# Gate norm vector folded into the gate weights, its root applied at the sigmoid, p loaded later, and a 19-buffer weight ring started earlier

## The chip, the cores and the metric

One Trainium2 chip, one core. The metric is device time in microseconds of one execution of the whole program. All arrays are float32 in HBM; nothing is prepared on the host.

## The reference, cut to what matters

One layer on 1024 tokens of width 1024. The token mixers ahead of the experts are not touched by the change and are left out here.

```python
def rmsnorm(x, g):
    return x * lax.rsqrt(jnp.mean(x * x, axis=-1, keepdims=True) + EPS) * g

def reference(x, p, norm_mix, w_in, ...):
    ...                                        # mixers; h = h + concat(y_lru, y_gdn) @ w_out
    h = h + hier_moe(rmsnorm(h, norm_ffn[l]), w_router_group[l], ..., w_exp_gate[l], w_exp_up[l], w_exp_down[l])
    gate = jax.nn.sigmoid(rmsnorm(h, norm_ple[l]) @ w_ple_gate[l])
    h = h + gate * (p[l] @ w_ple[l])
    return rmsnorm(h, norm_final)
```

`hier_moe` has 32 experts of 1024 to 512 to 1024 (silu gate times up, then down); each token goes to two of them. `norm_ple` is the vector that the change folds: `rmsnorm(h, g) @ W` is `(h @ (g[:, None] * W))` times one number per token, the reciprocal root.

## The kernel before

Tokens are in 8 tiles of 128 rows. Four stages matter here.

**Output projection and routing (to about 600 us).** For each token tile c the loop makes h, its norm (`ffn_xn`, which writes the normed rows to HBM as `xn_d`), the router's logits and its choice. SP issues the loads and stores of this stage in program order, one queue: the store of h (`h_d`), the store `xn_d`, and between them pieces of the experts' weights.

**The weight stream.** `halves` is a list of 198 pieces of 1 MB, in the order in which they are used: two gate and two up pieces of an expert, two down pieces, and at the end w_ple, p and four pieces of w_ple_gate. `raw_half(n)` (L1130) issues n of them on SP into a ring of buffers, `ring_tile()`. The ring has 18: 6, and from the output projection's end 9 more (`MORE`), and from the experts on 3 more (`LATE`). A DMA on SP waits until the DMA eight places ahead of it has landed, and for its buffer's last reader. The last tile's `ffn_xn` store and `raw_half(MORE - 1)` stand behind that tile's norm. Then SP, as the other engines, comes to a branch on a value that routing computes (`further`, L1404 and L1405), and waits there both for the value and for all of its own DMAs.

**Experts.** For expert e rows are gathered by GpSimd's indirect DMA (`gather`, L1222) out of `xn_d`, transposed, and multiplied by gate, up (L1314) and down pieces; results are scattered to `y_d` (L1280), row by row, one row per slot and token.

**The p stage and the gate stage.** `p_T` transposes a tile of p and splits it in a high and a low part; `parts(w)` does the same to weights (ScalarE copies to the rounded type fp32r, L1524, and VectorE subtracts, L1525); `mm3` (L205) multiplies high by high, low by high and high by low. For each tile, `p @ w_ple` comes first, kept in ring buffers. In between, the tail reads the two expert results of each token (`y_load`), adds them (`y_sum`, L1615, on GpSimd but for tile 0), adds h (`y_add`, L1619), squares with a sum (`y_sq`, ScalarE L1625) and applies the norm (`y_norm`: a Newton root, L43 to L53, and L1631, which multiplies by the root and the vector gple). `split_T` (L1293 to L1295) transposes the result and splits it; per tile two half products follow (`gated`: sigmoid L1688, times p's product on GpSimd L1689; `added` L1692; `squared` L1695; and `last`, the final norm, with L1706 and the store). Within a tile's first half VectorE also runs `last` of the tile before, the split of the next tile and `y_norm` of the tile two further on.

From the output projection on, the engines' orders are written by hand; only the first stage is ordered by a scheduler.

Of the kernel before, what the change touches and what calls it, by code (L numbers as in the profile page):

```python
# [37 lines left out]

def newton_rsqrt(nc, pool, x, n, tag):

    r = pool.tile([P, n], F32, tag=tag + "_r")
    t = pool.tile([P, n + (n == 1)], F32, tag=tag + "_t")
    nc.vector.tensor_scalar(r.bitcast(I32), x.bitcast(I32), -0.5, 0x5F3759DF, op0=OP.mult, op1=OP.add)  # L43
    if n == 1:
        t, m = t[:, 0:1], t[:, 1:2]
        nc.vector.tensor_scalar(m, x, -0.5, None, op0=OP.mult)
    for _ in range(3):
        if n == 1:
            nc.vector.scalar_tensor_tensor(t, r, m, r, op0=OP.mult, op1=OP.mult)  # L49
# [34 lines left out]
def layer(ctx, tc, x, p, norm_mix, w_in, lru_conv_w, lru_conv_b, lru_wa, lru_ba, lru_wi, lru_bi,  # L84
# [70 lines left out]
    for k in range(0, KT, 2):  # L155
# [3 lines left out]
    VEC = ((lru_conv_w, 16), (gdn_conv_w, 48), (lru_conv_b, 4), (lru_ba, 4), (lru_bi, 4), (lru_lambda, 4),  # L159
           (lru_out_norm, 4), (gdn_out_norm, 1), (norm_ffn, 8))  # L160
    NV = sum(n for _, n in VEC)
    vrow = zp.tile([NV, P], F32, name="vrow")
    r0, vecs = 0, []
    for a, n in VEC:
# [4 lines left out]
    cvg = vec[:, 16:64].rearrange("p (j g) -> p j g", j=4)  # L169
    cvb, ba_, bi_, lam, lon, gon, gfc = (vec[:, 64:68], vec[:, 68:72], vec[:, 72:76], vec[:, 76:80],  # L170
                                         vec[:, 80:84], vec[:, 84:85], vec[:, 85:93])
    alog = cst.tile([P, NH], F32, name="alog")
# [791 lines left out]

    def ffn_xn(c, eng):
        xn, ht = xns[c], by_tile(prepared[c][2])
        xk, gk = (a.rearrange("p (k q) -> p k q", k=KT) for a in (xn, gffn))
        if eng is nc.scalar:
            eng.activation(xk, ht, AF.Copy, scale=rss[c])
            nc.gpsimd.tensor_mul(xn, xn, gffn)  # L970
        else:
            eng.scalar_tensor_tensor(xk, ht, rss[c], gk, op0=OP.mult, op1=OP.mult)
        nc.sync.dma_start(xn_d[c * P:(c + 1) * P, :], xn)

# [131 lines left out]
    for e in range(NE + 1):  # L1106
# [3 lines left out]
        if e == NE - 1:  # L1110
            halves += [wpe, p[0, 0].rearrange("(t p) c -> p t c", p=P)]
        if e > 0:
            halves += [wd_v[EXPERTS[e - 1], :, 2 * j:2 * j + 2, :] for j in range(2)]
    halves += [wpg[:, 2 * i:2 * i + 2, :] for i in range(4)]
    halves.reverse()
# [90 lines left out]
    ffn_logits(c, 1)  # L1206
    raw_half()
    ffn_lgs(c)
    step(cur, 2)
    ffn_xn(c, nc.vector)  # L1210
    raw_half(MORE - 1)
    r = route(c - 1, c + 1)
# [72 lines left out]

    def split_T(pool, src, n, tag, bufs=2, size=0):

        th = pool.tile([P, size or n, P], F32R, tag=tag + "h", bufs=bufs)
        tl = pool.tile([P, size or n, P], F32R, tag=tag + "l", bufs=bufs)
        for k0 in range(0, n, 4):  # L1290
# [74 lines left out]
    mo = ctx.enter_context(tc.tile_pool(name="mo", bufs=2, reuse_waits="tile"))  # L1365
    LATE = 3
    ring[0:0] = [(mo, f"w{i}") for i in range(LATE)]
# [139 lines left out]
    def p_T():  # L1507

        t = len(pp)
        if t % 4 == 0:  # L1510
            pr[:] = [mo.tile([P, KT, P], F32R, tag="x" + c, bufs=2, name="pt") for c in "hl"]
        ph, pl = (x[:, 2 * (t % 4):2 * (t % 4) + 2] for x in pr)
# [7 lines left out]

    def parts(w):

        wh, wl = ring_tile(F32R), ring_tile(F32R)
        nc.scalar.activation(wh, w, AF.Copy)  # L1524
        nc.vector.tensor_sub(wl, w, wh)  # L1525
        return wh, wl

# [3 lines left out]
    for e in range(NE + 1):  # L1531
# [49 lines left out]
        if e == NE - 1:  # L1581
            gple = xg2[0]
            nc.sync.dma_start(gple, bcast_rows(norm_ple, D))
            we = [a.rearrange("p (k c) -> p k c", k=2) for a in parts(wpr)]
            hr = ring_tile()
            for t in range(2):
                hs[t] = hr[:, t * D:(t + 1) * D]
                nc.sync.dma_start(hs[t], h_d[t])
            for t in range(4):
                p_T()  # L1590
    mst.close()
# [3 lines left out]

    with tc.tile_pool(name="tl", bufs=2, reuse_waits="tile") as tl:
        gfin = xg2[1]
        nc.sync.dma_start(gfin, bcast_rows(norm_final, D))
# [3 lines left out]
        y0s, y1s, sss, x2s = {}, {}, {}, {}  # L1602
        yr = None

        def y_load(t):
            if t < NT:
                y0 = tl.tile([P, D], F32, tag="y0", bufs=3)
                y1 = yr[:, (t % 2) * D:(t % 2) * D + D]
                y0s[t], y1s[t] = y0, y1
                for m, y in enumerate((y0, y1)):  # L1610
                    nc.sync.dma_start(y, y_d[m * S + t * P:m * S + (t + 1) * P, :])
# [14 lines left out]

        def y_norm(t):
            if t < NT:
                nc.vector.tensor_scalar(sss[t], sss[t], EPS, None, op0=OP.add)
                rs = newton_rsqrt(nc, sm, sss[t], 1, "nx")  # L1630
                nc.vector.scalar_tensor_tensor(y0s[t], hs[t], rs, gple, op0=OP.mult, op1=OP.mult)  # L1631

        for t in range(NT):
            if t < 4:
                p_T()
            ph, pl = pp[t]
            if t % 2 == 0:
                w = ring_tile()
                if t == 0:
                    yr = ring_tile()  # L1640
                pws[t], pws[t + 1] = w[:, 0:D], w[:, D:]
# [7 lines left out]
            if t == 0:  # L1649
                y_load(0)  # L1650
                y_load(1)
            if t in (1, 2, 3, 4):
                gw.append([a.rearrange("p (k c) -> p k c", k=2) for a in parts(wgr[t - 1])])
            if t == 4:
                y_sum(0, nc.vector)
                y_add(0)
                y_sq(0)
                y_sum(1)
                y_load(2)
            if t == 5:  # L1660
                y_norm(0)
        for t in range(2, NT, 2):
            w = ring_tile()
            for j in range(2):
                hs[t + j] = w[:, j * D:(j + 1) * D]
                nc.sync.dma_start(hs[t + j], h_d[t + j])
        x2s[0] = split_T(mo, y0s[0], KT, "x")
        y_load(3)
        y_add(1)
        y_sq(1)  # L1670
        y_sum(2)
        y_norm(1)
        y_add(2)
# [8 lines left out]
        def gated(t, n, ns, pg):  # L1682
# [4 lines left out]
            sg = sgs[t, n] = sg[:, 0:ns.stop - ns.start]  # L1687
            nc.scalar.activation(sg, pg, AF.Sigmoid)  # L1688
            (nc.vector if (t, n) >= (NT - 1, 1) else nc.gpsimd).tensor_mul(sg, sg, pws[t][:, ns])  # L1689
# [27 lines left out]
        for t in range(NT):  # L1717
            xh, xl = x2s[t]
            for n, ns in enumerate(pieces(t)):
# [4 lines left out]
                if n == 0:  # L1724
                    if t > 0:
                        last(t - 1)
                    if t + 1 < NT:
                        x2s[t + 1] = split_T(mo, y0s[t + 1], KT, "x")
                    y_load(t + 4)
                    added(t, 0, ns)  # L1730
                    y_norm(t + 2)
                    y_sum(t + 3)
# [39 lines left out]
```

## Time and profile before

| what | value |
|---|---|
| three runs | 1301.15, 1294.4, 1297.95 us |
| median | 1297.95 us |
| profiled execution, its own time | 1297.76 us |
| its span | 1296.1 us |
| mean granted TensorE clock | 0.962 |

The span is the time from the first to the last instruction in the trace; 1.66 us of the execution's time lie around it. Positions in the text are microseconds from the span's start. The busy lines give for each engine its busy time, share and count; the line of 40 slices gives one digit for each 32.4 us.

### The profile page before, as it was taken

Reading aid. Unit: us, or ns where it says so; the run is one execution under the profiler, and the core shown is the slowest. Engines: PE = TensorE matmul, PEld = TensorE weight load, DVE = VectorE, ACT = ScalarE, POOL = GpSimd, SP = SyncE. Lnnn points to the kernel's source line nnn. Section 1 sums busy time; section 2 is a strip of 40 time slices with the busy share of each in tenths; the row PEclk is TensorE's granted clock in tenths of the full one; section 3 lists DMA queues with packets and bytes.
Section 4 is the critical chain, followed back from the end, with each engine's and each line's share of the span. In section 5 each row is a group of like instructions: output and inputs, shape, how many; then the busy total and the mean of one; then the engine's idle time right before and its main releaser. Section 6 shows DMA issues by size and latency. Waiting matters only on the chain. (4 is left out here: it accounts for less than half of the span.)

```text
span 1296.1 us, 17798 instructions
## 1 busy us (share of the span) xinstructions
PE 1188.2 (92%) x6295; PEld 736.7 (57%) x6295; DVE 698.4 (54%) x1462; ACT 407.0 (31%) x691; POOL 265.5 (20%) x232
## 2 busy tenths in 40 slices
PE   6999979999889999975999999999999899998886
PEld 5987757776679988863333333333333333366665
DVE  7657766779878986883222212222222122266885
ACT  5423436654423234431121111111121122254232
POOL 2121224542141202221011111111111101012322
PEclk9999989999979999976999999999999999998998
DMA  6711121330544446668999999999999999864221
GB/s 206 251 33 50 36 54 66 98 82 0 151 132 147 147 145 214 247 231 352 401 398 397 384 401 389 399 390 395 395 397 390 377 392 404 351 249 174 98 82 49
DMA packets 98204, 309.43 MB, mean 239 GB/s; under 512 B 23423, under 2 KB 45020, under 8 KB 73501
## 3 DMA queue, kind: packets, MB, share of 16 engines
q1 hardware_dynamic: 91740, 290.74, 60.4%
q0 software_dynamic: 6336, 17.05, 3.9%
q8 instruction: 74, 1.21, 0.4%
q14 instruction: 54, 0.43, 0.1%
HBM read 273.28 MB, written 38.54 MB: 241 GB/s over the span
## 5 line engine op out<-in xcount | busy, mean ns | idle before, releaser
L1314 PE MATMUL b<-w,x 128*64 128x512 f32 x1024 | 235.8, 602 | 11.4 <-PEq L1545 4.7
L1314 PEld LDWEIGHTS b<-w,x 128*64 128x64 f32 x1024 | 72.6, 137 | 149.2 <-issue 141.3
L1314 PE MATMUL b<-w,h 128*64 128x512 f32 x512 | 124.2, 604 | 3.6 <-PEq L1567 2.9
L1326 DVE SCALAR_TENSOR_TENSOR gs<-gs,gts,b 64x512 f32<-64x512 f32 x32 | 23.7, 739 | 151.0 <-ACT gs L1325 144.2
L205 PE MATMUL b<-xh,wh 128*128 128x512 f32 x320 | 85.9, 411 | 0.0
L1222 POOL DMA_INDIRECT xg<-xn_d,idx x32 | 31.0, 969 | 263.9 <-PE b L1485 243.3
L205 PE MATMUL b<-xh,wl 128*128 128x512 f32 x320 | 79.2, 390 | 0.0
L205 PE MATMUL b<-xl,wh 128*128 128x512 f32 x320 | 79.0, 389 | 0.0
L1280 POOL DMA_INDIRECT y_d<-y,idx x32 | 29.5, 921 | 225.3 <-ACTq L1545 123.3
L286 POOL TENSOR_TENSOR wl<-w,wh 128x1024 fp32r<-128x1024 f32 x20 | 52.7, 2637 | 104.2 <-ACT wh L285 101.0
L1314 PEld LDWEIGHTS b<-w,h 128*64 128x64 f32 x512 | 33.2, 136 | 70.2 <-issue 55.4
L205 PEld LDWEIGHTS b<-xh,wh 128*128 128x128 f32 x320 | 61.9, 195 | 15.4 <-issue 1.7
L205 PEld LDWEIGHTS b<-xh,wl 128*128 128x128 f32 x320 | 60.3, 189 | 12.7
L205 PEld LDWEIGHTS b<-xl,wh 128*128 128x128 f32 x320 | 60.1, 188 | 12.5
L205 PE MATMUL b<-w,th 128*128 128x512 f32 (+1 forms) x272 | 66.0, 390 | 0.0
L1325 ACT ACTIVATE gs<-b 64x512 f32<-64x512 f32 x32 | 19.0, 595 | 126.6 <-PE b L1314 126.6
L1352 DVE TENSOR_TENSOR gs<-b,gs 32x512 f32<-32x512 f32 x13 | 8.9, 685 | 89.8 <-ACT yo L1351 89.8
L205 PEld LDWEIGHTS b<-w,th 128*128 128x128 f32 x272 | 49.6, 192 | 10.9 <-ACT th L1294 0.2
L1332 ACT ACTIVATE y<-b 64x512 f32<-64x512 f32 x32 | 19.0, 594 | 111.7 <-DVE y L1331 83.2
L1342 PE MATMUL b<-w,x 128*32 128x512 f32 x416 | 50.0, 598 | 3.3 <-PEq L1539 3.3
L1331 DVE COPY y<-b 64x512 f32<-64x512 f32 x32 | 21.9, 683 | 53.6 <-PE b L1314 50.1
L355 DVE SCALAR_TENSOR_TENSOR kq<-pre,vec,kq 128x1024 f32<-128x1024 f32 x24 | 47.0, 1958 | 0.9
(392 smaller groups left out, 2180.8 us busy)
## 6 DMA issues: line engine op xcount, KB each, us to landing
w<-in_w_exp_gate_dram SPq DMA_DIRECT2D x64, 1024.0 KB
w<-in_w_exp_up_dram SPq DMA_DIRECT2D x64, 1024.0 KB
w<-in_w_exp_down_dram SPq DMA_DIRECT2D x64, 1024.0 KB
w<-in_w_in_dram SPq DMA_DIRECT2D x20, 512.0 KB
xt<-in_x_dram SPq DMA_DIRECT2D x16, 512.0 KB
h_d<-xt SPq DMA_DIRECT2D x8, 512.0 KB
ht<-h_d SPq DMA_DIRECT2D x8, 512.0 KB
h_d<-ht SPq DMA_DIRECT2D x8, 512.0 KB
```

Source lines behind the costliest of these rows:

```text
L205: nc.tensor.matmul(o, a(k), b(k), start=(i == 0), stop=(i == 3 * n - 1))
L286: nc.gpsimd.tensor_sub(wl, raw[i], wh)
L355: nc.vector.scalar_tensor_tensor(dst, pre[:, t0 + j:t0 + j + n], w[:, j, g:g + 1], dst, op0=OP.mult, op1=OP.add)
L1222: nc.gpsimd.indirect_dma_start(out=xg[rows], out_offset=None, in_=xn_d[:], in_offset=bass.IndirectOffsetOnAxis(ap=idx[rows], axis=0), boun ...
L1280: i = nc.gpsimd.indirect_dma_start(out=y_d[:], out_offset=bass.IndirectOffsetOnAxis(ap=idx[rows], axis=0), in_=y[rows], in_offset=None, bo ...
L1314: nc.tensor.matmul(pb[rows], xT[:, k], of(k, m), start=(k == 0), stop=(k == n - 1))
L1325: nc.scalar.activation(dst, pb[other(r)], AF.Silu)
L1326: nc.vector.scalar_tensor_tensor(dst, dst, gt, pb[r], op0=OP.mult, op1=OP.mult)
L1331: nc.vector.tensor_copy(y[:, 0:512], pb[r])
L1332: nc.scalar.activation(y[:, 512:], pb[other(r)], AF.Copy)
L1342: nc.tensor.matmul(pb[32 * j:32 * j + 32], xT[:, k], of(k, m), start=(k < 2), stop=(k >= n - 2), tile_position=(0, 32 * j))
L1352: nc.vector.tensor_add(dst, pb[32:64], dst)
```

## The change

- `raw_half(MORE)` issues its nine pieces right behind the last tile's transposes, ahead of that tile's logits and norm; before, one piece stood behind the logits and eight behind the norm's store. The last tile's `xn_d` store is issued by ScalarE's queue in place of SP's.
- `LATE` is 4: the ring has 19 buffers. The room comes from the low parts (`xl`), which go to the tail's pool.
- p stands behind the last down pieces in the stream; its transposes are no longer inside the last expert's code but three ahead of the p stage and one in each of its tiles.
- `norm_ple` is loaded as columns (`gpl`) and applied when w_ple_gate is split: `parts(w, g)` runs two scaled copies on ScalarE and two scalar_tensor_tensor on VectorE of 1024 columns for each piece, where there was one of each of 2048. The broadcast of the vector to 128 rows (0.5 MB, L1583) is gone. The splits stand at tiles 0, 1, 4, 5 instead of 1 to 4.
- `y_norm` becomes `y_rs`: the root alone. L1631 is gone; `split_T` reads h itself, and the root is the sigmoid's scale on ScalarE.
- The expert results of a tile go to ring buffers, three pairs; `y_sum(0)` and `y_add(0)` move from the p stage's tile 4 to tile 2, `y_sq(0)` to 3, `y_sum(1)` to 5.

```diff
@@ ffn_xn
-    def ffn_xn(c, eng):
+    def ffn_xn(c, eng, queue=nc.sync):
...
-        nc.sync.dma_start(xn_d[c * P:(c + 1) * P, :], xn)
+        queue.dma_start(xn_d[c * P:(c + 1) * P, :], xn)
@@ halves
         if e == NE - 1:
-            halves += [wpe, p[0, 0].rearrange("(t p) c -> p t c", p=P)]
+            halves.append(wpe)
         if e > 0:
             halves += [wd_v[EXPERTS[e - 1], :, 2 * j:2 * j + 2, :] for j in range(2)]
+    halves.append(p[0, 0].rearrange("(t p) c -> p t c", p=P))
@@ end of the output projection
     for t in xg2:
         nc.gpsimd.memset(t, 0.0)
+    raw_half(MORE)
     step(cur)
...
     ffn_logits(c, 1)
-    raw_half()
     ffn_lgs(c)
     step(cur, 2)
-    ffn_xn(c, nc.vector)
-    raw_half(MORE - 1)
+    ffn_xn(c, nc.vector, nc.scalar)
@@ ring
-    LATE = 3
+    LATE = 4
@@ parts
-    def parts(w):
+    def parts(w, g=None):
         wh, wl = ring_tile(F32R), ring_tile(F32R)
-        nc.scalar.activation(wh, w, AF.Copy)
-        nc.vector.tensor_sub(wl, w, wh)
-        return wh, wl
+        if g is None:
+            nc.scalar.activation(wh, w, AF.Copy)
+            nc.vector.tensor_sub(wl, w, wh)
+        else:
+            for k in range(2):
+                ks = slice(k * D, k * D + D)
+                nc.scalar.activation(wh[:, ks], w[:, ks], AF.Copy, scale=g[:, k:k + 1])
+                nc.vector.scalar_tensor_tensor(wl[:, ks], w[:, ks], g[:, k:k + 1], wh[:, ks],
+                                               op0=OP.mult, op1=OP.subtract)
+        return [a.rearrange("p (k c) -> p k c", k=2) for a in (wh, wl)]
@@ tail
-        def y_norm(t):
+        def y_rs(t):
             if t < NT:
                 nc.vector.tensor_scalar(sss[t], sss[t], EPS, None, op0=OP.add)
-                rs = newton_rsqrt(nc, sm, sss[t], 1, "nx")
-                nc.vector.scalar_tensor_tensor(y0s[t], hs[t], rs, gple, op0=OP.mult, op1=OP.mult)
+                sss[t] = newton_rsqrt(nc, tl, sss[t], 1, "ny", bufs=4)
...
-            if t in (1, 2, 3, 4):
-                gw.append([a.rearrange("p (k c) -> p k c", k=2) for a in parts(wgr[t - 1])])
-            if t == 4:
+            if t in (0, 1, 4, 5):
+                i = len(gw)
+                gw.append(parts(wgr[i], gpl[:, 2 * i:2 * i + 2]))
+            if t == 2:
                 y_sum(0, nc.vector)
                 y_add(0)
+                y_load(2)
+            if t == 3:
                 y_sq(0)
+            if t == 5:
                 y_sum(1)
-                y_load(2)
-            if t == 5:
-                y_norm(0)
...
-        x2s[0] = split_T(mo, y0s[0], KT, "x")
+        x2s[0] = split_T(hs[0])
+        y_rs(0)
...
-            nc.scalar.activation(sg, pg, AF.Sigmoid)
+            nc.scalar.activation(sg, pg, AF.Sigmoid, scale=sss[t])
```

SP at the end of the output projection, before (`xn_d<-xn` is the store of normed rows, `w<-in_w_exp...` a piece of weights, L1404 the value that the branch waits for):

```order
L973 DMA xn_d<-xn 128x1024
L930 DMA h_d<-ht 128x1024
L1130 DMA w<-in_w_exp_gate_dram 128x2048
L973 DMA xn_d<-xn 128x1024
L1130 DMA w<-in_w_exp_up_dram 128x2048
L1130 DMA w<-in_w_exp_down_dram 128x2048 x2
L1130 DMA w<-in_w_exp_gate_dram 128x2048
L1130 DMA w<-in_w_exp_up_dram 128x2048
L1130 DMA w<-in_w_exp_gate_dram 128x2048
L1130 DMA w<-in_w_exp_up_dram 128x2048
L1130 DMA w<-in_w_exp_down_dram 128x2048
L1404 TENSOR_LOAD novi
```

The same place of SP now:

```order
L973 DMA xn_d<-xn 128x1024
L930 DMA h_d<-ht 128x1024
L1131 DMA w<-in_w_exp_gate_dram 128x2048
L1131 DMA w<-in_w_exp_up_dram 128x2048
L1131 DMA w<-in_w_exp_down_dram 128x2048 x2
L1131 DMA w<-in_w_exp_gate_dram 128x2048
L1131 DMA w<-in_w_exp_up_dram 128x2048
L1131 DMA w<-in_w_exp_gate_dram 128x2048
L1131 DMA w<-in_w_exp_up_dram 128x2048
L1131 DMA w<-in_w_exp_down_dram 128x2048
L1407 TENSOR_LOAD novi
```

The last store of normed rows no longer stands between the pieces; it is on ScalarE's queue.

VectorE through the p stage and into the gate stage, before (L1518 is p's low part, L1525 a weight's low part, L1615 and L1619 `y_sum(0)` and `y_add(0)`):

```order
L1518 TENSOR_TENSOR pt<-b,pt 128x256
L1525 TENSOR_TENSOR w<-w 128x2048
L1518 TENSOR_TENSOR pt<-b,pt 128x256
L1525 TENSOR_TENSOR w<-w 128x2048
L1518 TENSOR_TENSOR pt<-b,pt 128x256
L1525 TENSOR_TENSOR w<-w 128x2048 x2
L1615 TENSOR_TENSOR y_11680<-y_11680,w 128x1024
L1619 TENSOR_TENSOR w<-w,y_11680 128x1024
L1629 TENSOR_SCALAR ss<-ss 128x1
```

The same stretch of VectorE now (L1521 and L1534 are the low parts, L1625 and L1629 `y_sum(0)` and `y_add(0)`, L1298 the low part of tile 0):

```order
L1521 TENSOR_TENSOR xl<-b,xh 128x256 x4
L1534 SCALAR_TENSOR_TENSOR w<-w,vec 128x1024 x2
L1521 TENSOR_TENSOR xl<-b,xh 128x256
L1534 SCALAR_TENSOR_TENSOR w<-w,vec 128x1024 x2
L1521 TENSOR_TENSOR xl<-b,xh 128x256
L1625 TENSOR_TENSOR w<-w 128x1024
L1629 TENSOR_TENSOR w<-w 128x1024
L1521 TENSOR_TENSOR xl<-b,xh 128x256 x2
L1534 SCALAR_TENSOR_TENSOR w<-w,vec 128x1024 x4
L1298 TENSOR_TENSOR xl<-b,xh 128x512 x2
```

Tile 0's sum stands ahead of the second pair of weight splits, and its split (L1298) comes ahead of its root, with no norm in front of it.

VectorE inside one tile of the gate stage, from the end of the root to the next tile's final norm, before (L1631 is the norm of the gate's input, L1619 `y_add`, L1692 `added`, L1697 the final norm's mean; numbers behind a name are buffers):

```order
L53 SCALAR_TENSOR_TENSOR r<-t,r 128x1
L1631 SCALAR_TENSOR_TENSOR y_11877<-w,r,xg_5118 128x1024
L1619 TENSOR_TENSOR w<-w,y_11944 128x1024
L1692 TENSOR_TENSOR w<-w,sg 128x512
L1697 SCALAR_TENSOR_TENSOR ss<-ss 128x1
```

And now:

```order
L53 SCALAR_TENSOR_TENSOR r<-t,r 128x1
L1629 TENSOR_TENSOR w<-w 128x1024
L1701 TENSOR_TENSOR w<-w,sg 128x512
L1706 SCALAR_TENSOR_TENSOR ss<-ss 128x1
L43 TENSOR_SCALAR r<-ss 128x1
```

The multiply of 128x1024 is gone; the rest of the tile keeps its order.

## Rows read from the trace of the kernel before

**Rows 1.** The page, parts 1 and 2: busy time of TensorE and VectorE over the span, and in 40 slices the granted clock and the DMA share, in tenths.

```profile
PE 1188.2 (92%) x6295; PEld 736.7 (57%) x6295; DVE 698.4 (54%) x1462; ACT 407.0 (31%) x691; POOL 265.5 (20%) x232
...
PEclk9999989999979999976999999999999999998998
DMA  6711121330544446668999999999999999864221
```

**Rows 2.** Busy time by stretch, two answers of the windows view: columns are the stretch, its length, busy time of PE, PEld, DVE, ACT and POOL with counts, granted clock, DMA share, GB/s.

```profile
570.00:579.00 9.00, 7.33 (x32) 6.98 (x32) 6.50 (x29) 0.20 (x1) 0.89 (x2) 0.50 0.64 231
579.00:583.00 4.00, 0.00 (x0) 0.00 (x0) 3.52 (x21) 0.21 (x1) 0.00 (x0) 0.50 0.90 291
583.00:600.00 17.00, 7.17 (x32) 6.92 (x32) 10.79 (x53) 0.20 (x1) 4.12 (x5) 0.50 1.01 419
```

```profile
900.00:1000.00 100.00, 96.74 (x515) 32.93 (x512) 25.51 (x40) 20.14 (x36) 12.23 (x13) 1.00 1.02 395
1140.50:1165.00 24.50, 23.71 (x105) 18.69 (x104) 16.60 (x16) 14.34 (x19) 3.30 (x2) 1.00 0.56 214
1165.00:1175.00 10.00, 2.41 (x10) 2.11 (x11) 6.55 (x12) 5.10 (x10) 2.34 (x1) 0.61 0.91 356
1181.44:1193.90 12.46, 12.25 (x58) 9.72 (x57) 8.56 (x15) 5.22 (x9) 4.95 (x3) 1.00 0.24 84
1193.90:1208.90 15.00, 12.54 (x56) 9.69 (x57) 13.21 (x26) 4.43 (x10) 4.94 (x3) 1.00 0.30 105
1238.78:1253.73 14.95, 12.54 (x57) 9.69 (x57) 13.16 (x26) 4.43 (x10) 4.96 (x3) 1.00 0.09 37
1253.73:1266.56 12.83, 12.26 (x56) 9.75 (x57) 11.04 (x26) 4.43 (x10) 2.59 (x2) 1.00 0.10 41
```

**Rows 3.** SP's timeline ahead of the experts: start, length, what is issued. The length of a group of two runs to the end of the second.

```profile
569.97 0.78 SPq L1130 DMA_DIRECT2D w<-in_w_exp_gate_dram  x1
578.62 0.32 SPq L973 DMA_DIRECT2D xn_d<-xn  x1
...
583.36 24.22 SPq L1130 DMA_DIRECT2D w<-in_w_exp_down_dram  x2
607.70 0.35 SPq L1130 DMA_DIRECT2D w<-in_w_exp_gate_dram  x1
```

**Rows 4.** What SP's queue waits for from 560 to 615 us: who waits, for whom, us in total, times, longest.

```profile
SPq L1405 <- SPq L1405: 12.6, 3, 5.6
...
SPq L973 <- DVE xn L972: 7.8, 1, 7.8
```

**Rows 5.** What TensorE waits for from 600 to 1150 us, same columns.

```profile
PE b L1485 <- DMA xg<-xn_d,idx: 10.4, 1, 10.4
...
PE b L1314 <- DMA w<-in_w_exp_up_dram: 4.4, 3, 3.3
```

**Rows 6.** TensorE's timeline late in the experts, two of those waits: start, length, instruction, in brackets the idle time before it and what ended it.

```profile
1008.48 1.08 PE L1314 MATMUL b<-w,x 128*64 128x512 f32 x4 [3.26 <-DMA w<-in_w_exp_up_dram]
```

```profile
1026.21 1.08 PE L1314 MATMUL b<-w,x 128*64 128x512 f32 x4 [0.95 <-DMA w<-in_w_exp_up_dram]
```

**Rows 7.** GpSimd's timeline: the first gather; and of the DMA view of 565 to 610 us the gathers' median time from issue to landing, in us.

```profile
591.20 1.16 POOL L1222 DMA_INDIRECT xg<-xn_d,idx  x1 [20.31 <-DVE nb L1255]
```

```profile
xg<-xn_d,idx POOLq DMA_INDIRECT x3, 9.3
```

**Rows 8.** VectorE's timeline from the p stage into the gate stage.

```profile
1156.29 2.29 DVE L1525 TENSOR_TENSOR w<-w 128x2048 fp32r<-128x2048 f32 x1 [0.42 <-ACT w L1524]
1159.07 4.54 DVE L1525 TENSOR_TENSOR w<-w 128x2048 fp32r<-128x2048 f32 x1 [0.49 <-ACT w L1524]
1163.53 1.21 DVE L1615 TENSOR_TENSOR y<-y,w 128x1024 f32<-128x1024 f32 x1
...
1171.16 1.28 DVE L1631 SCALAR_TENSOR_TENSOR y<-w,r,xg 128x1024 f32<-128x1024 f32 x1
...
1196.80 0.16 DVE L1697 SCALAR_TENSOR_TENSOR ss<-ss 128x1 f32<-128x1 f32 x1 [1.23 <-ACT b L1695]
```

**Rows 9.** TensorE's timeline from the last p product to the second gate product.

```profile
1162.73 2.26 PE L205 MATMUL b<-w,pt 128*128 128x512 f32 x9
1172.59 1.94 PE L1293 MATMUL b<-ident,y 128*128 128x128 f32 x8 [7.60 <-DVE y L1631]
1174.37 3.50 PE L205 MATMUL b<-w,th 128*128 128x512 f32 x8
...
1181.44 1.04 PE L1293 MATMUL b<-ident,y 128*128 128x128 f32 x8
1182.23 2.11 PE L205 MATMUL b<-w,th 128*128 128x512 f32 x8
1184.18 2.03 PE L205 MATMUL b<-w,tl 128*128 128x512 f32 x8
```

**Rows 10.** GpSimd's timeline in the p stage: the sum of tile 1's expert results; and TensorE's: a pair of p's transposes in the last expert.

```profile
1159.06 2.39 POOL L1615 TENSOR_TENSOR y<-y,w 128x1024 f32<-128x1024 f32 x1 [14.06 <-DMA w<-y_d]
```

```profile
1141.28 0.44 PE L1515 MATMUL b<-ident,w 128*128 128x128 f32 x2 [0.78 <-DVE pt L1518]
```

**Rows 11.** What TensorE waits for from 1181 to 1285 us, the gate stage without its start.

```profile
PE b L1293 <- DVE y L1631: 6.0, 6, 1.3
PE b L205 <- DVE tl L1295: 4.5, 4, 1.2
```

More of the change, by code (lines that the diff above doesn't have):

```diff
@@ L36, with newton_rsqrt @@
 ORDERED = {mybir.EngineType.PE, mybir.EngineType.Activation, mybir.EngineType.DVE, mybir.EngineType.Pool}
-def newton_rsqrt(nc, pool, x, n, tag):
-    r = pool.tile([P, n], F32, tag=tag + "_r")
+def newton_rsqrt(nc, pool, x, n, tag, bufs=2):
+    r = pool.tile([P, n], F32, tag=tag + "_r", bufs=bufs)
     t = pool.tile([P, n + (n == 1)], F32, tag=tag + "_t")
@@ L159, in layer @@
     VEC = ((lru_conv_w, 16), (gdn_conv_w, 48), (lru_conv_b, 4), (lru_ba, 4), (lru_bi, 4), (lru_lambda, 4),
-           (lru_out_norm, 4), (gdn_out_norm, 1), (norm_ffn, 8))
+           (lru_out_norm, 4), (gdn_out_norm, 1), (norm_ffn, 8), (norm_ple, 8))
     NV = sum(n for _, n in VEC)
@@ L169, in layer @@
     cvg = vec[:, 16:64].rearrange("p (j g) -> p j g", j=4)
-    cvb, ba_, bi_, lam, lon, gon, gfc = (vec[:, 64:68], vec[:, 68:72], vec[:, 72:76], vec[:, 76:80],
-                                         vec[:, 80:84], vec[:, 84:85], vec[:, 85:93])
+    cvb, ba_, bi_, lam, lon, gon, gfc, gpl = (vec[:, 64:68], vec[:, 68:72], vec[:, 72:76], vec[:, 76:80],
+                                              vec[:, 80:84], vec[:, 84:85], vec[:, 85:93], vec[:, 93:101])
     alog = cst.tile([P, NH], F32, name="alog")
@@ L1284, in scatter, with high_low, split_T @@
         scat.append(i)
-    def split_T(pool, src, n, tag, bufs=2, size=0):
-        th = pool.tile([P, size or n, P], F32R, tag=tag + "h", bufs=bufs)
-        tl = pool.tile([P, size or n, P], F32R, tag=tag + "l", bufs=bufs)
+    def high_low():
+        return (mo.tile([P, KT, P], F32R, tag="xh", name="xh"), lo_p.tile([P, KT, P], F32R, tag="xl", name="xl"))
+    def split_T(src):
+        n = KT
+        th, tl = high_low()
         for k0 in range(0, n, 4):
@@ L1510, in p_T @@
         if t % 4 == 0:
-            pr[:] = [mo.tile([P, KT, P], F32R, tag="x" + c, bufs=2, name="pt") for c in "hl"]
+            pr[:] = high_low()
         ph, pl = (x[:, 2 * (t % 4):2 * (t % 4) + 2] for x in pr)
@@ L1555, in layer @@
         if e == NE - 1:
-            wpr, praw = next_raw(2)
+            (wpr,) = next_raw(1)
         if e > 0:
@@ L1581, in layer @@
         if e == NE - 1:
-            gple = xg2[0]
-            nc.sync.dma_start(gple, bcast_rows(norm_ple, D))
-            we = [a.rearrange("p (k c) -> p k c", k=2) for a in parts(wpr)]
+            we = parts(wpr)
             hr = ring_tile()
@@ L1588, in layer @@
                 nc.sync.dma_start(hs[t], h_d[t])
-            for t in range(4):
-                p_T()
     mst.close()
@@ L1596, in layer @@
     with tc.tile_pool(name="tl", bufs=2, reuse_waits="tile") as tl:
+        lo_p = tl
+        (praw,) = next_raw(1)
+        for _ in range(3):
+            p_T()
         gfin = xg2[1]
@@ L1602, in layer @@
         y0s, y1s, sss, x2s = {}, {}, {}, {}
-        yr = None
+        yt = {}
         def y_load(t):
             if t < NT:
[L1607 to L1610, printed above, removed]
+                if t < 3:
+                    yt[t] = ring_tile()
+                y0s[t], y1s[t] = yt[t % 3][:, 0:D], yt[t % 3][:, D:]
+                for m, y in enumerate((y0s[t], y1s[t])):
                     nc.sync.dma_start(y, y_d[m * S + t * P:m * S + (t + 1) * P, :])
@@ L1625, in y_sq @@
                 nc.scalar.activation(y0s[t], hs[t], AF.Square, scale=D ** -0.5, accum_out=ss)
-        def y_norm(t):
+        def y_rs(t):
             if t < NT:
                 nc.vector.tensor_scalar(sss[t], sss[t], EPS, None, op0=OP.add)
-                rs = newton_rsqrt(nc, sm, sss[t], 1, "nx")
-                nc.vector.scalar_tensor_tensor(y0s[t], hs[t], rs, gple, op0=OP.mult, op1=OP.mult)
+                sss[t] = newton_rsqrt(nc, tl, sss[t], 1, "ny", bufs=4)
         for t in range(NT):
-            if t < 4:
+            if t + 3 < NT:
                 p_T()
@@ L1638, in layer @@
                 w = ring_tile()
-                if t == 0:
-                    yr = ring_tile()
                 pws[t], pws[t + 1] = w[:, 0:D], w[:, D:]
@@ L1671, in layer @@
         y_sum(2)
-        y_norm(1)
+        y_rs(1)
         y_add(2)
@@ L1727, in layer @@
                     if t + 1 < NT:
-                        x2s[t + 1] = split_T(mo, y0s[t + 1], KT, "x")
+                        x2s[t + 1] = split_T(hs[t + 1])
                     y_load(t + 4)
                     added(t, 0, ns)
-                    y_norm(t + 2)
+                    y_rs(t + 2)
                     y_sum(t + 3)
```

## The prediction

> **What bounds the kernel now.** The page comes first: TensorE is busy 92% of the span, and the slices give the places where its clock or the DMA share falls [rows 1]. Two lie where the change works: around 560 to 610 us (slices 18 and 19) and near the end. The windows give each stretch its own limit. In the experts TensorE is busy 96.74 of 100 us while the DMA engines are full (share 1.02, 395 GB/s) [rows 2]: the matmuls and the weight stream run at the same pace, and a piece that lands late stops TensorE. In the p stage TensorE is busy 23.71 of 24.5 us. Between 1165 and 1175 us it works 2.41 of 10. In the gate stage a tile takes 14.95 us with 12.54 of TensorE and 13.16 of VectorE, but 12.46 in the first, undisturbed tile [rows 2]: there VectorE sets the pace. Nothing before 560 us carries a term: the scheduler there exchanges a few short neighbours, and one small load is added.
>
> All sums are against the profiled execution, 1297.76 us; the three runs' median, 1297.95, is 0.19 away, and I treat them as one. 0.5% is 6.5 us, about what a measurement can tell from no change.
>
> **Part 1, the stream begins earlier.** SP issues a piece at 569.97 and the next thing only at 578.62, the store of the last normed rows [rows 3]: it waited 7.8 us for VectorE's norm [rows 4], and eight pieces stood behind it. The store is now on ScalarE, so the pieces go out as soon as the DMA eight places ahead lands. How much sooner the ninth lands is worked out from the DMA rate: it was 231 GB/s for 9 us and 291 for 4, then 419 [rows 2]. At 419 throughout, 9 x (1 - 231/419) + 4 x (1 - 291/419) = 4.0 + 1.2 = 5.3 us of transfer move ahead. Behind the ninth SP waits at the branch for all its own DMAs, and only at about 607.6 does the next piece go out (583.36 + 24.22) [rows 3, 4]; that wait has the same end, earlier by the same 5.3, because the value that decides the branch was there long before. The lead is then carried through the experts, since the stream ran at its limit (share 1.02) and the ring now has one buffer more. The upper end is the whole 7.8 us, the lower end 2.5 (half, if transfers already on the way and the gathers fill the gap).
>
> What the lead is worth: TensorE waited 4.4 us in all for weights, 3.26 and 0.95 of it at 1008 and 1026 us [rows 5, 6]. At the start of the experts weights are not what it waits for, but the gather (10.4 us) [rows 5], which hangs on routing, so nothing is won there. A lead of 5.3 covers all 4.4; one of 2.5 gives 2.5. **Gain 4.4 us, 2.5 to 4.4.** The 0.5 MB broadcast that goes and p's later place (the slot of a last down piece, which had to be there sooner) cost nothing on the path; cover is that stream's lead, and p late would stop TensorE at the p stage by a piece, 2.7 us (1.05 MB at 395 GB/s).
>
> **Part 2, the start of the gate stage.** Before, p's last product ended at 1165.0, and TensorE then stood 7.60 us until L1631 had normed tile 0; its transposes began at 1172.59 and the first half product ended at 1181.44, eight matmuls of it 3.50 us long against 2.03 at the full clock [rows 9]; the granted clock of 1165 to 1175 was 0.61 [rows 2]. The chain behind it was a weight's low part that took 4.54 instead of 2.29 us beside GpSimd's 2.39 us sum, then `y_sum`, `y_add`, square, root, L1631 [rows 8, 10]. Now the sum for tile 0 stands two tiles earlier, and the transposes need h alone. VectorE reaches `y_sum(0)` ahead of the expert results' landing and waits; what is queued behind it is p's low parts for tiles 6 and 7, whose products come three tiles later. GpSimd began tile 1's sum at 1159.06, released by its landing [rows 10], and tile 0's results are loaded first: two adds of 1.21 us from there, 1161.5, bound tile 0's h, ahead of the end of p's products. That end moves to 1166.2, as three of p's transposes no longer hide in the last expert: 0.44 us for a pair and 0.78 for its low part [rows 10] are 1.2. Transposes and split as before, 1.8 us (1172.59 to 1174.37), then 24 matmuls at the full clock, 2.11 + 2.03 and a third group like the second, less overlaps, 5.6 us: the end is 1173.6 instead of 1181.44. **Gain 7.8.** The added work, eight scalar_tensor_tensor of 1024 columns at L1631's 1.28 us instead of four subtractions of 2.29, is 10.2 against 9.2 us on VectorE, which had 7.9 us free in the p stage [rows 2, 8]; two of these pairs now meet GpSimd's sum for tile 1 and can be stretched by 2.3 us, as the 4.54 us one was. That takes up to 3: **5 to 9.** ScalarE's scaled copies hide (14.34 busy of 24.5).
>
> **Part 3, the loop of the gate stage.** In four tiles VectorE also adds a later tile's experts. TensorE stops 10.5 us in all, half at the transposes for L1631 and half at the low part behind it [rows 11]; four periods of about 14.95 against 12.46 are 9.9 us, and the later 12.83 ones 0.4 each. L1631 (1.28, of which 1.20 are net since starts overlap) goes from every tile [rows 8]. VectorE's period then is 13.75 with all its idle time kept (of which 1.23 is a wait for ScalarE's square), 11.9 without it. Against 12.46 it falls behind by at most 1.3 a tile, 5.2 in four tiles; in the first tile, though, it has 3.9 us free (12.46 - 8.56) [rows 2]. That leaves some 1.5 us of stops: **gain 9, from 4.8 (4 x 1.20) to 10.9.** The root as a scale costs ScalarE little, and it is busy 4.43 of 14.95 us; the chain after the last product is unchanged.
>
> **Sum:** 4.4 + 7.8 + 9 = 21.2, 1297.76 - 21.2 = 1276.56, said as 1276.5. Ends of the terms together: 12.3 to 24.3, 1273.5 to 1285.5.
>
> **Rivals.**
> A: GpSimd's sums stretch the new splits and VectorE stays the bound. The start gains 2.3 less, 5.5, the loop 4.8: with 4.4, 14.7 us, 1283. For it: 4.54 against 2.29 us beside GpSimd's 2.39 [rows 8, 10]; against it: VectorE's free time in the p stage and the 1.23 us in the loop, which can take such a stretch in. The Trainium skill, SBUF — State Buffer, section "SBUF: two separate sides", says why the row is as it is: a VectorE instruction with two SBUF inputs and a GpSimd one lock each other out for the whole instruction. By it the new splits, with two such inputs, are caught whenever they meet the sum, and the start gives 5.5; by the free time alone it gives 7.8, and with that I stay.
>
> B: the store of the normed rows on ScalarE's queue is served only behind the nine pieces ahead of it, by about 601 us. The gather before was issued at 591.20 and took 9.3 [rows 7]; it would land at 610, and the experts begin 9.3 later: 1276.5 + 9.3 = 1285.8. Against it: that gather itself landed in 9.3 us while six pieces on SP's queue were under way until 607 [rows 3, 7], so one queue doesn't keep another out. The Trainium skill, DMA: Bandwidth & Descriptors, "Queues, rings and completion order", has each DMA engine take turns between queues packet by packet; by this the store lands within a few us and B does not occur. The trace agrees so far as the gather's 9.3 goes; no row shows a store on ScalarE's queue.
>
> C: the change does not give the lead. The pieces wait for buffers or landings in the same gap, and the stream reaches 1008 us as late as before: no 4.4, 1280.9.
>
> D, the slower side: B's service in order holds for the gathers as well, so that the first one waits behind the store and then behind the eight pieces that SP issues after the branch: 601 + 9.3 + 8 x 2.7 = 632 us instead of 600.5, 31 us, 1307.9. It makes the kernel slower than before as soon as the gather lands later than 622 us (600.5 + 21.2). The same row that speaks against B speaks against it twice.
>
> **How the numbers follow.** Forecast 0.57 (1271 to 1281), A 0.16, B 0.09, C 0.09, D 0.04, and 0.05 for pairs such as A with B (1292.4). Predicted is the likeliest, 1276.5. The range of 1267.5 to 1288 takes in A, B, C and the upper ends of all terms with some us for what no row bounds, and leaves D and the pairs out. Faster by over 0.5% (below 1291.5) 0.88, within 0.5% 0.08 (the pairs and part of D), slower by over 0.5% 0.04.
>
> **What would show it.** Part 1: SP issues nine pieces from about 570 us without a store in between, the next one after the branch at about 602, the first gather still lands near 600.5, and TensorE waits for weights under 1 us in the experts. Part 2: the idle time of 7.60 us before the gate's first transposes is under 1.5, with the clock at 1.00 throughout. Part 3: L1631's row is missing, the period of a gate tile is near 12.5 to 13, and waits for VectorE in the loop are 1 to 5 us in all. It would be wrong if the store's landing moved the first gather, if a weight split on VectorE ended after 1171 us, or if the loop's period stayed above 13.7.

## The result, and the profile after

| | before | after |
|---|---|---|
| median of four runs | 1299.19 us | 1280.82 us (1278.3 to 1281.83) |
| ratio, with its 95% interval | | 0.9868 (0.984 to 0.9895) |
| span of the profiled execution | 1296.1 us | 1280.1 us |

The change makes the kernel 1.3% faster, 18 us by the medians and 16.0 by the two profiles' spans. 1276.5 was predicted, 4.3 us below the median; the range held it.

The page of the kernel after, answering to [rows 1]: TensorE does the same work in a shorter span, and the low slice of the clock near the end (the 8 in the 37th) is gone.

```profile
PE 1186.1 (93%) x6295; PEld 736.3 (58%) x6295; DVE 686.8 (54%) x1458; ACT 409.8 (32%) x695; POOL 267.1 (21%) x232
...
PEclk9999979999969999995999999999999999999998
```

SP's timeline ahead of the experts, answering to [rows 3]:

```profile
570.43 0.78 SPq L1131 DMA_DIRECT2D w<-in_w_exp_gate_dram  x1
571.26 1.18 SPq L1131 DMA_DIRECT2D w<-in_w_exp_up_dram  x1
...
580.84 20.91 SPq L1131 DMA_DIRECT2D w<-in_w_exp_down_dram  x2
601.87 0.35 SPq L1131 DMA_DIRECT2D w<-in_w_exp_gate_dram  x1
```

The second piece goes out at 571.26 instead of 578.98 and the one behind the branch ends at 601.75 (580.84 + 20.91) instead of 607.58: the stream leads by 5.8 us. What TensorE waits for from 596 to 1150 us, answering to [rows 5]:

```profile
PE b L1488 <- DMA xg<-xn_d,idx: 9.7, 1, 9.7
...
PE b L1317 <- DMA w<-in_w_exp_up_dram: 1.1, 1, 1.1
```

The gather is not later (its first transposes come at 600.47, before at 600.64), and 1.1 of 4.4 us of these waits for weights are left; two further profiles of the changed kernel have 2.2 and 0.2. TensorE's timeline into the gate stage, answering to [rows 9]:

```profile
1162.24 0.62 PE L205 MATMUL b<-w,xh 128*128 128x512 f32 x2
1162.70 1.04 PE L1296 MATMUL b<-ident,w 128*128 128x128 f32 x8
1164.58 2.14 PE L205 MATMUL b<-w,xh 128*128 128x512 f32 x8 [0.84 <-ACT xh L1297]
...
1170.25 1.03 PE L1296 MATMUL b<-ident,w 128*128 128x128 f32 x8
...
1182.21 1.04 PE L1296 MATMUL b<-ident,w 128*128 128x128 f32 x8
...
1193.04 2.14 PE L205 MATMUL b<-w,xl 128*128 128x512 f32 x8 [2.38 <-DVE xl L1298]
```

The stop of 7.60 us ahead of the first transposes is gone. Behind them stands one of 0.84 us for ScalarE's copy, and the next matmuls run at the full clock (2.14 us for eight, not 3.50; 1.00 granted from 1160 to 1175). In the loop a stop of 2.38 us stands at the low part. The windows of the gate stage, columns as in [rows 2], and the waits of TensorE from 1130 to 1285 us, answering to [rows 11]:

```profile
1170.25:1182.21 11.96, 11.96 (x58) 9.84 (x56) 7.94 (x16) 5.40 (x9) 4.93 (x3) 1.00 0.73 293
1182.21:1196.87 14.66, 12.28 (x58) 9.78 (x57) 12.77 (x29) 4.61 (x10) 4.90 (x4) 1.00 0.25 82
1196.87:1210.65 13.78, 12.24 (x57) 9.76 (x56) 12.03 (x25) 4.61 (x10) 4.93 (x4) 1.00 0.34 117
...
1238.27:1250.23 11.96, 11.96 (x58) 9.84 (x56) 10.19 (x26) 4.61 (x10) 2.72 (x3) 1.00 0.11 44
```

```profile
PE b L205 <- DVE xl L1298: 7.1, 4, 2.4
```

A tile without stops takes 11.96 us. Four, called heavy from here on, still have one (2.38, 1.54, 1.58 and 1.55 us); the first of them takes 14.66 us, the others 13.8. The stops are all at the same instruction: VectorE's low part of the next tile. VectorE's timeline ahead of the first of them:

```profile
1171.54 1.22 DVE L1629 TENSOR_TENSOR w<-w 128x1024 f32<-128x1024 f32 x1
1176.47 1.29 DVE L1298 TENSOR_TENSOR xl<-b,xh 128x512 fp32r<-128x512 f32 x2 [3.71 <-ACT xh L1297]
...
1186.83 1.23 DVE L53 SCALAR_TENSOR_TENSOR r<-t,r 128x1 f32<-128x1 f32 x1
1188.09 2.32 DVE L49 SCALAR_TENSOR_TENSOR t<-r,t 128x1 f32<-128x1 f32 x1
...
1192.30 1.28 DVE L1298 TENSOR_TENSOR xl<-b,xh 128x512 fp32r<-128x512 f32 x2
```

It stood idle for 3.71 us before tile 1's low part, waiting for ScalarE's copy, and ahead of tile 2's it spent 1.23 and 2.32 us in steps on 128 numbers that elsewhere take 0.16 and 0.22. ScalarE's and GpSimd's timelines at these two places:

```profile
1172.80 1.06 ACT L1635 ACTIVATE w<-w 128x1024 f32<-128x1024 f32 x1 [2.96 <-DVE w L1629]
...
1173.97 1.28 ACT L1697 ACT_TABLE_LOAD   x1
1175.26 0.69 ACT L1697 ACTIVATE sg<-b,r 128x512 f32<-128x512 f32 x1
1175.85 1.08 ACT L1297 ACTIVATE xh<-b 128x512 fp32r<-128x512 f32 x2
```

```profile
1186.74 1.30 POOL L1698 TENSOR_TENSOR sg<-sg,w 128x512 f32<-128x512 f32 x1 [4.51 <-ACT sg L1697]
1188.00 2.40 POOL L1625 TENSOR_TENSOR w<-w 128x1024 f32<-128x1024 f32 x1
```

ScalarE's copy stood behind a square, a table load and the sigmoid; VectorE's long steps begin within 0.1 us of GpSimd's two instructions and end with them.

The landmarks for a sum by stages are TensorE's last down product and its last matmul, before and then after:

```profile
1138.57 1.94 PE L1314 MATMUL b<-w,h 128*64 128x512 f32 x8 [0.16 <-PEq L1567]
...
1283.48 1.11 PE L205 MATMUL b<-w,th 128*128 128x256 f32 x8
```

```profile
1133.15 4.02 PE L1317 MATMUL b<-w,h 128*64 128x512 f32 x16 [1.48 <-issue]
...
1266.96 1.10 PE L205 MATMUL b<-w,xh 128*128 128x256 f32 x8
```

Stage by stage, in these two profiles: the last down product ends at 1140.51 before and 1137.17 after, 3.3 us earlier. From there to the second tile's transposes it is 40.93 and 33.08 us (1181.44 and 1170.25), a gain of 7.9. From those to TensorE's end 103.15 and 97.81, 5.3. Behind TensorE's end 11.5 and 12.0, a loss of 0.5. Sum 16.0.

### The profile page after: what moved, and what is told of

It is laid out like the page before. It is cut to its first block, busy times and chain, and to the rows that moved or that the text cites. A ratio compares the mean times of both kernels' runs of the same rounds, so it can differ in the third digit from the quotient of the medians.

```text
span 1280.1 us, 17777 instructions
## 1 busy us (share of the span) xinstructions
PE 1186.1 (93%) x6295; PEld 736.3 (58%) x6295; DVE 686.8 (54%) x1458; ACT 409.8 (32%) x695; POOL 267.1 (21%) x232
## 5 line engine op out<-in xcount | busy, mean ns | idle before, releaser
L205 PE MATMUL b<-w,xh 128*128 128x512 f32 (+1 forms) x336 | 82.5, 386 | 2.2 <-ACT xh L1520 1.4
L205 PEld LDWEIGHTS b<-w,xh 128*128 128x128 f32 x336 | 60.2, 188 | 14.9 <-ACT xh L1520 1.6
L205 PE MATMUL b<-w,xl 128*128 128x512 f32 (+1 forms) x168 | 42.8, 385 | 7.1 <-DVE xl L1298 7.1
```

What stands on the lines that cost most here:

```text
L205: nc.tensor.matmul(o, a(k), b(k), start=(i == 0), stop=(i == 3 * n - 1))
```

## The experiments

My theory is that of the prediction, three gains that add up, with one amendment from the profile after: in the loop VectorE's sequence still sets the pace, through its stretched steps beside GpSimd. Times are medians, each with the ratio to runs of the kernel before taken beside it. One thing is needed to read them: executions differ by some 6 us in where the experts begin. In the profiles of e2_stream_back, e2_again and e12 the clock granted from 520 to 560 us was 1.00, and TensorE's first transposes of gathered rows came at 594.3 to 595.9. In all other profiles it was 0.96 to 0.99, and they came at 599.4 to 602.1 (e3, which delays them, apart). That stretch lies ahead of the pieces that the change moves, so stages are compared by their lengths; whether the edits have a part in it is open.

**e1, the stream's part alone**, on the kernel before:

```diff
+    raw_half(MORE)          # behind the memsets of xg2
...
-    raw_half()
...
-    ffn_xn(c, nc.vector)
-    raw_half(MORE - 1)
+    ffn_xn(c, nc.vector, nc.scalar)
```

> The kernel before with the stream's part alone: nine pieces issued right behind the last transposes, the last store of normed rows on ScalarE's queue; ring of 18 buffers, tail as before. Theory: the pieces land 4 to 5 us earlier, TensorE's 4.4 us of waits for weights in the experts fall to about 1, the p stage begins 3.3 us earlier, and the time falls by 3.3 us against the kernel before (about 1296), with the 7.6 us stop ahead of the gate stage unchanged. Rival 1: the lead needs the nineteenth buffer and is lost on the way with 18; then the waits for weights stay near 4 us and the time within 1 us of before. Rival 2: the early pieces delay the last store or the gathers; then the first expert's transposes begin later than 600.6 us.

1295.05 against 1300.88 us, ratio 0.9953 (0.9939 to 0.9968). TensorE's waits from 600 to 1150 us:

```profile
PE b L1484 <- DMA xg<-xn_d,idx: 9.7, 1, 9.7
...
PE b L1313 <- DMA w<-in_w_exp_up_dram: 0.2, 1, 0.2
```

The waits for weights are all but gone with 18 buffers (0.8 us in all), so the nineteenth is not what carries the lead, and the wait for the gather is no longer than before. The experts begin at 601.76, which is rival 2's sign, but the last tile's norm on VectorE was already 1.8 us later than before in this profile (578.23, 576.48 before), so the store and the gather did not add to it. From the first transposes of gathered rows to the last down product it took 536.4 us instead of 539.9. The time fell by 5.8 us, more than the 3.3 expected and than the 3.5 of that stage.

**e2, the stream back at its old place** in the changed kernel, first alone and then a second time beside the changed kernel:

```diff
-    raw_half(MORE)
...
+    raw_half()
     ffn_lgs(c)
     step(cur, 2)
-    ffn_xn(c, nc.vector, nc.scalar)
+    ffn_xn(c, nc.vector)
+    raw_half(MORE - 1)
```

> The changed kernel with the pieces and the store of normed rows back at their old places on SP; the ring keeps 19 buffers. Theory: the lead is gone, TensorE waits about 4.4 us for weights in the experts, the time is 3 to 4.5 us above the changed kernel (1284 to 1285), and gate stage and loop are as in the changed kernel (first half product 33.1 us behind the last down product, heavy tiles of 13.8 us). Rival: the nineteenth buffer alone gives the lead, and the time is within 1 us of the changed kernel.

1283.09 us, 0.987 (0.9854 to 0.9887). That fitted neither side: the waits for weights were back (3.8 us in one stop), yet the ratio was the changed kernel's. The first transposes of gathered rows came at 595.9 in that profile. Both kernels were then run side by side:

> The changed kernel again, beside the same kernel with the stream at its old place in the same call: 0.987 of the kernel before, within 0.2%.

> The changed kernel with the pieces and the store back at their old places, a second time and on the same chip as the changed kernel. Theory: 2 to 4 us above the changed kernel of this call, with 3.5 to 5 us of waits for weights in the experts against about 1. Rival: the same time within 1 us, because the stage ahead of the experts ends earlier without the early pieces (as in the first look, where the first gather landed at 596 us).

1282.08 us for the changed kernel, 0.9875 (0.9858 to 0.9891), and 1287.13 without its stream, 0.9907 (0.9892 to 0.9922): 5 us, and the intervals just miss each other. But the same kernel's ratio of 0.987 in e2_stream_back is as far from its 0.9907, so the whole times leave the price of the lead open between nothing and 5 us. TensorE's waits in e2_again's experts, and its first transposes of gathered rows:

```profile
PE b L1318 <- DMA w<-in_w_exp_up_dram: 4.9, 3, 4.1
PE b L1318 <- DMA w<-in_w_exp_down_dram: 1.2, 4, 0.3
```

```profile
594.29 1.51 PE L1489 MATMUL b<-ident,xg 96*128 96x96 f32 x8 [10.16 <-DMA xg<-xn_d,idx]
```

Experts that begin 6.7 us earlier end no earlier (1138.2): from there on they took 543.9 us (543.1 in e2_stream_back), in the changed kernel beside it 536.0. The early start is not the reason. e12 below has the lead and starts as early:

```profile
594.91 1.51 PE L1488 MATMUL b<-ident,xg 96*128 96x96 f32 x8 [10.09 <-DMA xg<-xn_d,idx]
```

It took 537.4 us. Of eleven profiles with the lead, ten lie at 535.6 to 538.0 us; the eleventh, e8, took 540.0. Without the lead the weights set the end of that stage. The changed kernel beside e5, e7 and e9 gave 1281.43 us, 0.988 (0.9857 to 0.9904):

> The changed kernel once more, for the direct comparison on one chip with the runs beside it: 0.987 of the kernel before, within 0.2%.

**e3, the store behind the pieces on one queue**: `ffn_xn(c, nc.vector, nc.scalar)` becomes `ffn_xn(c, nc.vector)`, the pieces stay early.

> The changed kernel with the last store of normed rows on SP's queue again, now behind the nine pieces. Theory: one queue is served in its order, so the store lands with or behind the ninth piece, about 602 us, the first gather behind it lands near 611, and TensorE begins the experts some 10 us later than at 600.5; minus the 1.1 us wait for weights that this hides, the time is 8 to 10 us above the changed kernel (1289 to 1291). Rival: the store passes the pieces or is not what the gather waits for; the experts begin at 600.5 as before and the time is 1281 within 1 us.

1291.33 us, 0.9935 (0.9918 to 0.9951). SP's timeline, GpSimd's, and TensorE's first transposes of the experts:

```profile
581.62 0.33 SPq L973 DMA_DIRECT2D xn_d<-xn  x1
```

```profile
602.08 1.16 POOL L1222 DMA_INDIRECT xg<-xn_d,idx  x1 [30.18 <-SPq L1408]
```

```profile
610.93 1.51 PE L1488 MATMUL b<-ident,xg 96*128 96x96 f32 x8 [19.65 <-DMA xg<-xn_d,idx]
```

The store is issued at 581.62 and the gather only at 602.08, 10.4 us later than in the changed kernel (591.66), as the theory said. The profile has no row for the store's landing; it names SP's wait at the branch, L1408, as what released the gather. That the store held it follows from the edit, which moves nothing else. So rival B's price was about right for one queue; on two queues it isn't paid.

**e8, an idle multiply of 128x1024 behind each root** on VectorE:

```diff
                 sss[t] = newton_rsqrt(nc, tl, sss[t], 1, "ny", bufs=4)
+                nc.vector.scalar_tensor_tensor(y0s[t], hs[t], sss[t], gfin, op0=OP.mult, op1=OP.mult)
```

> The changed kernel with an idle multiply of 128x1024 put back on VectorE behind each root (its result is read by nobody and TensorE doesn't wait for it by data). Theory: VectorE's sequence sets the pace of the gate loop, so the heavy tiles go from 13.8 to 15.0 us and the time rises by 4 to 6 us (1285 to 1287). Rival: what the change took off the path was the wait of the transposes for the normed tile, and VectorE has room; then the time rises by under 1 us.

1292.11 us, 0.9927 (0.9906 to 0.9947), where the changed kernel had 0.9868, 0.9875 and 0.988: some 6 to 8 us more, where 4 to 6 were expected. Its profile is of the longest of its four runs (1295.61). From the second tile's transposes to TensorE's end it was 106.55 us there instead of 97.81, 8.7 more. Of these 5.0 are stops (12.1 us in all instead of 7.1); the rest lies mostly in two tiles with a granted clock of 0.89 and 0.90, where TensorE was busy for 13.8 us instead of some 12. The last tile but one, by the windows:

```profile
1249.49:1262.52 13.03, 12.26 (x58) 9.77 (x57) 11.24 (x26) 4.61 (x10) 2.60 (x3) 1.00 0.10 40
```

It has a stop again (0.77 us; 13.03 against 11.96). An instruction that nobody waits for by data lengthens TensorE's stops, so VectorE's sequence is the bound there. How much of this is the multiply's own length, and how much is where it pushes other instructions against GpSimd's, the run does not separate; its experts were longer too (540.0 us), which the edit does not explain.

**e5, sums on VectorE; e7, sums and gate products on VectorE**:

```diff
-        def y_sum(t, eng=nc.gpsimd):
+        def y_sum(t, eng=nc.vector):
...                                   # e7 alone:
-            (nc.vector if (t, n) >= (NT - 1, 1) else nc.gpsimd).tensor_mul(sg, sg, pws[t][:, ns])
+            nc.vector.tensor_mul(sg, sg, pws[t][:, ns])
```

> The changed kernel with all sums of expert results on VectorE instead of GpSimd. Theory: a small root step of VectorE that meets GpSimd's 2.4 us sum takes 2.32 instead of 0.22 us, since the two engines keep each other out; the sum itself is 1.22 us on VectorE, so a heavy tile goes from 13.8 to 12.9 us, and the time falls by 3 to 4 us against the changed kernel. Rival: VectorE is bound by its own work and the long steps are waiting that costs nothing; then 1.22 us more a tile raises the time by 4 to 6 us.

> The changed kernel with the sums and the products of the gate with p's product on VectorE, nothing of the gate loop on GpSimd but the last tile's. Theory: in a heavy tile of 13.8 us the stretched root steps cost 2.1 + 1.1 + 1.1 = 4.3 us, and the work that moves is 1.22 + 2 x 0.68 = 2.6 us; the tile goes to about 12.1 us, TensorE stops under 1.5 us in the loop instead of 7.1, and the time falls by 5 to 7 us against the changed kernel. Rival: own work counts in full; then the tile goes to 16 us and the time rises by 10 us.

e5: 1276.88 us, 0.9836 (0.9812 to 0.9859); e7: 1271.79 us, 0.9797 (0.9775 to 0.9819), beside 1281.43 of the changed kernel. The gains are 4.6 and 9.6 us, more than the 3 to 4 and 5 to 7 expected. Tiles of both by the windows, then VectorE's timeline in e7:

```profile
1206.65:1219.62 12.97, 12.25 (x57) 9.77 (x56) 11.18 (x26) 4.61 (x10) 2.61 (x3) 1.00 0.35 120
```

```profile
1182.87:1194.85 11.98, 11.98 (x57) 9.85 (x56) 10.16 (x28) 4.73 (x10) 0.00 (x0) 1.00 0.38 129
1194.85:1206.81 11.96, 11.96 (x57) 9.84 (x56) 10.14 (x28) 4.73 (x10) 0.00 (x0) 1.00 0.38 130
```

```profile
1191.99 0.22 DVE L49 SCALAR_TENSOR_TENSOR t<-r,t 128x1 f32<-128x1 f32 x1
...
1192.77 1.23 DVE L1625 TENSOR_TENSOR w<-w 128x1024 f32<-128x1024 f32 x1
...
1195.17 0.68 DVE L1698 TENSOR_TENSOR sg<-sg,w 128x512 f32<-128x512 f32 x1
```

In e7 VectorE has more work and is less busy: 10.15 of 11.96 us against 12.03 of 13.78. With GpSimd silent, every root step takes 0.16 or 0.22 us, and TensorE has no stop in the loop. The version beats both kernels.

**e9, the split ahead of the sigmoid and the final norm; e11, the same with e7's edits**: `x2s[t + 1] = split_T(hs[t + 1])` moves ahead of `gated(t, n, ns, pg)`.

> The changed kernel with the next tile's split ahead of the sigmoid on ScalarE and ahead of the final norm of the tile before on VectorE; the work is the same. Theory: the low part no longer stands behind VectorE's root steps, and VectorE's 3.7 us wait at the loop's entry for ScalarE's copy (behind a table load and the sigmoid) goes; TensorE's 7.1 us of stops for the low part fall to 2 to 4, as VectorE is still slower a tile (13.8) than TensorE (12.0) but has half a tile of room; the time falls by 3 to 5 us against the changed kernel. Rival: only VectorE's total a tile counts; then the stops move to another place and the time is within 1 us.

> Sums and products on VectorE as in e7, and the split ahead of the sigmoid and the final norm. Theory: TensorE already ran without a stop in e7's loop (periods of 11.96), so the time is within 1 us of e7, 0.980 of the kernel before. Rival: the order still matters to what follows the last product (the end after TensorE was 12.6 us in e7 and 14.8 with the split first), and the time is 1 to 3 us above e7's.

e9: 1282.26 us, 0.9878 (0.9856 to 0.99), no gain. The low part no longer stops TensorE, but the waits went to ScalarE's copy and to the end. TensorE's waits after 1130 us, and the window behind its last product:

```profile
PE b L205 <- ACT xh L1297: 5.4, 5, 1.6
```

```profile
1267.13:1281.90 14.77, 0.00 (x0) 0.00 (x0) 6.36 (x17) 3.18 (x9) 2.71 (x3) 0.57 0.18 71
```

The 14.77 us were 12.0 in the changed kernel, with 6.36 us of VectorE's work instead of 4.87: its backlog comes out behind the loop. The first two tiles of the loop had no stop (11.98 and 11.96 us), the later heavy ones took 13.8 as before. The rival held. e11: 1272.04 us, 0.9788 (0.9773 to 0.9803), the same as e7 within the intervals, as its theory said.

**e12, tile 0's sum late**: `y_sum(0)`, `y_add(0)`, `y_sq(0)`, `y_sum(1)` and `y_load(2)` all at tile 5 of the p stage, behind the weight splits.

> The changed kernel with tile 0's sum, add and square, tile 1's sum and the third load of expert results after tile 5 of the p stage, behind all weight splits of VectorE. Theory: tile 0's h comes behind the four splits, some 2 to 4 us after p's last product; TensorE stops for that ahead of the gate stage, and the time rises by 2 to 4 us. Rival: what counted was the norm's chain alone (square, root, multiply); h is ready by p's end wherever the sum stands, and the time is within 1 us.

1282.61 us, 0.9879 (0.9861 to 0.9898): by time no difference that can be told. By the profile there is one. TensorE's timeline at the gate stage's start:

```profile
1161.05 1.06 PE L1296 MATMUL b<-ident,w 128*128 128x128 f32 x8 [3.04 <-DVE w L1629]
1164.57 3.78 PE L205 MATMUL b<-w,xh 128*128 128x512 f32 x8 [2.46 <-ACT xh L1297]
```

A stop of 3.04 us for the sum, 2.46 for ScalarE's copy, then eight matmuls in 3.78 us instead of 2.14, partly at the lower of the clock's two levels (0.68 granted from 1165 to 1172.69). From the last down product to the second tile's transposes it took 40.35 us, as before the change (40.93); the loop gave 2.2 back, for a reason that no run isolates. From the last down product to TensorE's end that is 5.7 us more than in the changed kernel beside it (135.6 against 129.9). The span doesn't show it because the experts began at 594.91 in this profile, 6 us earlier than in the changed kernel beside it. Four of this kernel's six runs had the mean clock of this profile, 0.968, and none of the changed kernel's four did (0.962 to 0.964). Whether the edit has a part in that stays open.

## Why the prediction was right or wrong

**Part 1 (4.4 us).** Right in mechanism: pieces out from 570 us, the piece behind the branch 5.8 us earlier against 5.3 reckoned from DMA rates, the gather untouched. By its length the experts' stage gained 3.2 us in the profile after and 3.5 in e1, where 4.4 were said; whole times put the part at 5.8 in e1 and at nothing or 5 in e2, so they cannot price it. The step on the nineteenth buffer was needless: e1 has the lead without it. Rival C fell with e1. B and D fell with the profile after, where the gather is not later; e3 shows that B's price is real where the store shares the queue (10.4 us), and the gather's 9.3 us beside pieces under way had spoken against it on two. The Trainium skill, DMA: Bandwidth & Descriptors, "Queues, rings and completion order", has descriptors consumed in the order of each ring and turns taken between queues; both rows agree with it.

**Part 2 (7.8 us).** Right, and the clock's part too: 7.9 in the profile after, 8.4 in ten other profiles with the same p stage (32.5 us instead of 40.93). e12 adds what the sum hid: the place of tile 0's sum carries the gain together with the missing norm. With the norm gone but the sum late, the start is as long as before. The early sum with the norm kept was not run.

**Part 3 (9 us).** Here the prediction failed in size: the stage gave 5.3, near the lower end of 4.8, which was rival A's figure. One of its signs of being wrong came true, a period above 13.7: heavy tiles took 13.8. The term that was mis-sized is the "some 1.5 us of stops" that would be left; 7.1 were left. Two steps made it too small. The first is "in the first tile, though, it has 3.9 us free". That time was not room: VectorE's next instruction waited 3.71 us for ScalarE's copy, behind a square, a table load and the sigmoid. The second is "at most 1.3 a tile": VectorE fell behind by 1.85 (13.8 against 11.96), since a tile without stops takes 11.96 us, not 12.46. e9 shows that the first step alone was not the miss: there the wait is 1.70 us, the loop's first two tiles have no stop, and the backlog only comes out later. Order alone doesn't help. L1631's own part was right: heavy tiles went from 14.95 to 13.8 (1.15 against 1.20). Of the 5.3 us only 3.4 are fewer stops (10.5 to 7.1); the other 1.9 is shorter time between stops, which I had not reckoned with and which no run explains.

Rival A's first half did happen without harm: four weight splits took 7.77 us beside GpSimd's sums, where some 5.1 were due, but the p stage had the room. e5 and e7 show its second half, that GpSimd's instructions, not VectorE's work, made the period. The Trainium skill, SBUF — State Buffer, "SBUF: two separate sides", describes a lock that one engine holds for its whole instruction while the other blocks; the trace agrees (a step of 0.22 us took 2.32 beside a sum of 2.40).

**The end** lost 0.5 us that I had put at nothing.

**The total.** By the two profiles, 3.3 + 7.9 + 5.3 - 0.5 is 16.0 us where 21.2 was said, and the range held it because it took in the rivals A, B and C. That the measured 1280.82 is also rival C's 1280.9 is chance: C has no lead, and e1 and the profile after show one.

## What to carry to other kernels

Idle time of an engine is room only if the next instruction in its order is ready: ask what the next one waits for before a lag is charged to it. Where two engines stretch each other's instructions, moving work to the busier one can lower its busy time; look for tiny steps with long rows. A stage's length between two landmarks tells of an edit where whole times are blurred by what lies ahead of it.

## What the runs showed of the hardware that I had not expected

VectorE was less busy with more work: 10.15 us a tile with sums and products on it, 12.03 without. A sigmoid of 128x512 takes 0.69 us with a per-row scale and took 0.60 with a constant one. The Trainium skill, ScalarE: Activation LUTs, "What ACT_TABLE_LOAD costs", gives some 93 ns for such an operand, and the trace agrees. At the end of the kernel two sigmoids of 128x256 took 0.46 us each instead of 0.36, which can be at most 0.2 of the 0.5 us lost there; the rest is open.
